# Inverses of the delta rule's triangular matrices: block levels on TensorE in place of a 16x16 substitution on VectorE through DRAM

## The chip, the cores and the metric

The kernel runs on one core of a Trainium2 chip. The metric is the device time of one execution in microseconds, the median of some runs. Profiles and traces show one execution. TensorE does the matrix products, VectorE (DVE), ScalarE (ACT) and GpSimd (POOL) the rest, and SyncE (SP) issues most transfers.

## The reference

One step of a backbone of two layers, for 512 latent tokens and 128 context tokens of width 1024. Each layer projects the normed tokens, runs four mixers side by side (grouped-query attention, neighbourhood attention, a gated delta rule in both directions, latent attention), projects their outputs and adds a gated feed-forward net of width 2816. The change is in the delta rule. It works on chunks of 64 tokens; for each chunk, head and direction a unit triangular system of 64x64 is solved:

```
def gated_delta_chunked(q, k, v, beta, logd, s0):
    c = DN_CHUNK                                   # 64
    ...
    gcum = jnp.cumsum(gc, axis=-1)
    dmask = jnp.where(tril, jnp.exp(jnp.where(tril, gcum[..., :, None] - gcum[..., None, :], 0.0)), 0.0)
    kb = kc * bc[..., None]
    a = jnp.where(strict, jnp.einsum('nbhid,nbhjd->nbhij', kb, kc) * dmask, 0.0)
    rhs = jnp.concatenate([vc * bc[..., None], kb * jnp.exp(gcum)[..., None]], axis=-1)
    sol = lax.linalg.triangular_solve(a + jnp.eye(c, dtype=jnp.float32), rhs,
                                      left_side=True, lower=True, unit_diagonal=True)
    u, w = sol[..., :dv], sol[..., dv:]
    ...
    def step(s, xs):
        u_i, w_i, qk_i, qd_i, kd_i, gl_i = xs
        v_new = u_i - jnp.einsum('bhcd,bhde->bhce', w_i, s)
        o_i = jnp.einsum('bhcd,bhde->bhce', qd_i, s) + jnp.einsum('bhij,bhje->bhie', qk_i, v_new)
        s = s * gl_i[..., None, None] + jnp.einsum('bhcd,bhce->bhde', kd_i, v_new)
        return s, o_i
    s_fin, o = lax.scan(step, s0.astype(jnp.float32), (u, w, qk, q_dec, k_dec, g_last))
```

There are 10 chunks, 4 heads and 2 directions, so 80 such matrices in each layer. The backward direction is the forward one on flipped tokens, so its matrices are upper triangular in the kernel's token order.

## The kernel before

All tokens stand side by side (640 columns) with features on 128 partitions. Large products take their operands in two parts of reduced precision, three products for one (L362, `mm3`; the loops at L624 to L711): these are the dense products, on full 128x128 blocks (tiles `acc` and `tacc` in the trace). Weights come in pieces through SP's queue and are split by ScalarE (`whi`) and VectorE (`wlo`).

TensorE's instructions are written out in an order that is fixed when the kernel is built. `_Order` (L190) keeps coroutines with ranks; each yields the time from which it can go on, an event, or buffers that it takes, and of those that can go on the first in rank does. `spend` keeps a measure of the dense columns issued of late (`heat`); while it is below a threshold, dense coroutines go first (L254 to L260). `via` estimates when a chain of steps on other engines ends. These are the planner's own estimates and serve the order alone. The other engines are ordered by the framework, each runs its instructions strictly one after another.

In a layer the mixer (L1850) spawns the delta rule's chain with rank 0 (`delta_chain`, L781), the other projections with rank 2 (`rest`, L1895), the modulation of layer 0 with rank 0.4 (`trickle`, L1924, transfers `wmd`, tiles `mpart`, `msb`), and the norms of the other mixers, which start at the event `inv` (L842). Attention (L1932) waits for the chain's end, since it takes over its room, and the half of the projections that is left runs beside it.

The chain: the keys' features and their short convolution (`conv_steps`, L735); the gates (L876); for 5 pairs of chunks the matrices `M` (tile `dM`) by L988 in `chunk_matrices` (L954), transposed, one head's parity on each half of the partitions; then the inverses; then the scan over the chunks (L1155) in both directions at once, and the output (`delta_out`, L1242). The values' and queries' features are projected meanwhile (L836, L837).

The inverses before: `inverse16` (L1014) writes the diagonal blocks of 16 of all matrices to DRAM (tile `dinv`, 8 transfers at L1025), reads them back with a whole matrix on each partition (L1034, L1035), turns the upper ones over (L1036), eliminates in 15 steps of two products and two subtractions on VectorE (L1043, L1047), and carries the inverses back through DRAM into the tile `rt` (L1049 to L1053). `inverse` (L1058) goes on with blocks in three groups of 8, 8 and 4 pairs of chunk and head: from 16 to 32 by two sets of 32x32 products (`first`, `second`: tiles `invp`, `ivr`, `ivy`), and from 32 to 64 by two sets (`third`, `fourth`) whose result replaces `M`. Before each first set VectorE turns `rt` over by 32x32 blocks (L1078). One coroutine runs the three groups one after another in each set.

Of the kernel before, what the change touches and what calls it, by code (L numbers as in the profile page):

```python
# [11 lines left out]
F32 = mybir.dt.float32  # L12
# [15 lines left out]
L = 2  # L28
# [24 lines left out]
def _constants():  # L53
# [6 lines left out]
    c["eye16"] = np.broadcast_to(np.eye(16, dtype=np.float32).reshape(1, 256), (128, 256))  # L60
# [3 lines left out]
    c["lev"] = np.stack([np.where((j < 16) & (i >= 16), -1.0, 0.0), np.where((j >= 16) & (i < 16), -1.0, 0.0)], 1)  # L64
# [23 lines left out]
_CBASE = ("ident", "ubig", "ident2", "eye16", "dmask", "lev", "sel2", "namask")  # L88
# [6 lines left out]
def _layout(inp):  # L95
# [25 lines left out]
    # gate columns ordered (parity, a|b, dir, pair)  # L121
# [47 lines left out]
    # state: (l, dir, parity, dk, pair, dv)  # L169
# [20 lines left out]
class _Order:  # L190
    """Order of the tensor engine's instructions among coroutines. A coroutine yields the time from which it can go on,
    an event, or (name, count) of the buffers that it takes; of those that can go on, the first in rank does.
    Times are estimates and only order instructions."""
# [82 lines left out]
class _Banks:  # L276
    """PSUM banks of some pools by turns: for every tag a list of (pool, tag)."""
# [10 lines left out]
class _Build:  # L288
# [13 lines left out]

    def split(self, hi, lo, src):
# [3 lines left out]
    def weights(self, src, shape, pool=None, bufs=2, parts=None):  # L307
        """A piece of a weight matrix, in its two parts."""
# [12 lines left out]
    def spare(e, l, pool, n):  # L321
        """Room for the two parts of a piece of the FFN's last weights, where its other buffers are free by then."""
# [13 lines left out]
    def put(self, oh, k, a, src, view=None):  # L336
        """Two parts of a piece of the mixers' outputs, from token a on."""
# [44 lines left out]
    def setup(self):  # L382
# [25 lines left out]
        for k, sh in _PAR.items():  # L408
# [21 lines left out]
            "inv": self.dp.tile([L, 2, 2, 2, 20, 4, 256], F32, name="dinv"),  # L430
        }

# [53 lines left out]
    def modulate(self, f, pool):  # L486
        """A part of the modulation numbers left, by the vector engine: layer 0's last gate, then layer 1's."""
# [26 lines left out]
    def scales(self, l, which, ks=slice(0, KD)):  # L514
        """norm gain * (1 + scale) of a sub-layer."""
# [8 lines left out]
    def sumsq(self, x, k, hf, pool, i=None, eng=None):  # L524
        """Squares of feature tile k of one half of the tokens, added up (by GpSimd: but for the last)."""
# [13 lines left out]
    def rstd(self, hf, pool):  # L539
        """1 / rms of the tokens of a half (None: of all), on partitions."""  # L540
# [12 lines left out]
    def bcast(self, hf, r, ps):  # L553
        """The same on all partitions in PSUM: (group, first and last token, numbers)."""
# [5 lines left out]
    def norm_k(self, l, which, hf, k, x, rb, h, pool):  # L560
        """Feature tile k of a half, normed and modulated, in two parts."""
# [20 lines left out]
    def out_k(self, k, x, rb):  # L582
        """Feature tile k of a half, normed, to the output."""
# [9 lines left out]
    def hooked(gen, hooks):  # L593
        """A coroutine run through, with calls after some of its steps."""
# [11 lines left out]
    def plain(gen):  # L606
        """A coroutine run through at once."""
# [16 lines left out]
    def fm_group(self, srcs, rhs, ks, acc, ws=None, tags=("w", "w")):  # L624
        """Some fm_tiles, side by side over the contraction."""
# [45 lines left out]
    def half_steps(self, w, rhs, ks, h, acc, tag="fd"):  # L671
        """A half of an fm_tile, in one PSUM bank."""
# [108 lines left out]
    def delta_chain(self, l, h, S, dn, dt, ps, pd, first):  # L781
# [57 lines left out]
        for e in evs:  # L839
            yield e  # L840
# [1357 lines left out]
```

## Time and profile before

| | |
|---|---|
| time, median of 3 runs | 1983.79 us (1981.31 to 1987.83) |
| span of the profiled execution | 1987.7 us |
| TensorE busy | 1861.4 us, 94% |
| VectorE, ScalarE, GpSimd busy | 55%, 37%, 14% |
| mean granted clock of TensorE | 0.968 of 2.4 GHz |
| delta rule's chain, from a layer's blocks going to DRAM (L1025) to the last product of the inverse | 114.2 to 244.2 us in layer 0, 1097.6 to 1210.0 us in layer 1 |

Busy time is the sum of an engine's instructions; the granted clock is the share of full speed that TensorE had, which is at one of two levels at a time (2.4 and 1.2 GHz), so that a mean between 0.5 and 1 is a mix. Idle time before an instruction is given with what ended it.

### The profile page before, as it was taken

The numbers are of one execution on the slowest core, as the hardware profiler recorded it, in microseconds if no ns is written. First come the engines' busy times: TensorE is split into PE (matmuls) and PEld (weight loads), VectorE is DVE, ScalarE is ACT, GpSimd is POOL, SyncE is SP. The second block draws the span as 40 slices with busy tenths as digits, with TensorE's granted clock in tenths as the row PEclk, the third lists the DMA queues.
The fourth block names the chain that finished last, engine by engine and source line by source line (L and its number), as shares of the span: only waits on it lengthen the run. The fifth ranks groups of instructions, "written<-read, shape, count | busy, mean of one in ns | idle before, by whom it ended". The sixth has DMA issues, their size and how long they took to land.

```text
span 1987.7 us, 40377 instructions
## 1 busy us (share of the span) xinstructions
PE 1861.4 (94%) x16620; PEld 1756.2 (88%) x16620; DVE 1098.9 (55%) x2372; ACT 734.1 (37%) x1505; POOL 287.1 (14%) x470
## 2 busy tenths in 40 slices
PE   5988998899999999999999879889999999999997
PEld 4977787778899999999998878777889999999997
DVE  6565556677667557657565664567766232323344
ACT  4622123766542112212345323267655221221231
POOL 1120321233310000000033031123322000000001
PEclk9988799999999999999999898989999999999999
DMA  7334333142535435435422222213352222222231
GB/s 295 128 97 126 114 99 109 30 109 78 168 140 173 141 111 183 145 125 182 132 93 90 63 68 68 77 52 75 94 167 83 76 76 78 78 69 83 74 96 54
DMA packets 116520, 213.51 MB, mean 107 GB/s; under 512 B 44400, under 2 KB 64368, under 8 KB 116208
## 3 DMA queue, kind: packets, MB, share of 16 engines
q1 hardware_dynamic: 113520, 206.22, 33.0%
q0 software_dynamic: 2816, 4.72, 1.2%
q8 instruction: 130, 2.13, 0.4%
q14 instruction: 54, 0.44, 0.1%
HBM read 186.29 MB, written 19.89 MB: 104 GB/s over the span
## 4 chain that ended last, share of the span: by engine, by line
PE 76%; DVE 9%; DMA 6%; ACT 4%; issue 2%; POOL 1%; SPq 1%; DVEq 0%; ACTq 0%; POOLq 0%
PE acc L347 54%; PE tacc L347 6%; PE ptp L359 2%; PE pvo L347 2%; PE sc L347 2%; DVE wlo L305 1%; PE mpart L347 1%; PE invp L347 1%; DMA wst<-wout 1%; DMA ivw<-dinv 1%; ACT whi L304 1%; DMA wmd<-wmod 1%; ACT p L1284 1%; DMA wmd<-wmodT 1%; POOL ar L1423 1%
## 5 line engine op out<-in xcount | busy, mean ns | idle before, releaser
L347 PE MATMUL acc<-h,whi 128*128 128x256 f32 (+1 forms) x3520 | 683.7, 313 | 2.3 <-ACT h L570 1.4
L347 PEld LDWEIGHTS acc<-h,whi 128*128 128x128 f32 x3520 | 583.4, 191 | 10.0 <-issue 3.4
L304 ACT CAST whi<-wst 128x1024 fp32r<-128x1024 f32 (+3 forms) x210 | 203.5, 970 | 698.2 <-PE acc L347 654.5
L347 PE MATMUL acc<-h,wlo 128*128 128x256 f32 (+1 forms) x1760 | 415.4, 313 | 7.5 <-DVE wlo L305 7.5
L305 DVE TENSOR_TENSOR wlo<-wst,whi 128x1024 fp32r<-128x1024 f32 (+3 forms) x210 | 238.0, 1134 | 200.4 <-ACT whi L304 199.3
L347 PEld LDWEIGHTS acc<-h,wlo 128*128 128x128 f32 x1760 | 322.6, 191 | 10.7 <-DVE wlo L305 8.6
L347 PE MATMUL acc<-g,whi 128*128 128x256 f32 (+1 forms) x1128 | 216.7, 309 | 0.2 <-DVE g L305 0.2
L347 PEld LDWEIGHTS acc<-g,whi 128*128 128x128 f32 x1128 | 185.9, 188 | 0.4 <-DVE g L305 0.4
L537 POOL TENSOR_TENSOR sq<-sq 128x256 f32<-128x256 f32 (+1 forms) x48 | 48.7, 1014 | 923.8 <-ACT sq L531 923.3
L1800 DVE SCALAR_TENSOR_TENSOR x<-acc,mods,x 128x256 f32<-128x256 f32 (+1 forms) x144 | 55.6, 434 | 186.6 <-PE acc L347 186.5
L503 DVE SCALAR_TENSOR_TENSOR wmj<-wmd,cb 128x1024 f32<-128x1024 f32 x112 | 136.8, 1221 | 37.9 <-DMA wmd<-wmodT 36.6
L347 PE MATMUL tacc<-whi,h 128*128 128x256 f32 (+1 forms) x640 | 154.2, 322 | 1.4 <-issue 1.0
L347 PE MATMUL acc<-g,wlo 128*128 128x384 f32 (+1 forms) x564 | 135.2, 309 | 0.0
L347 PEld LDWEIGHTS tacc<-whi,h 128*128 128x128 f32 x640 | 114.7, 200 | 10.6 <-issue 6.2
L347 PE MATMUL acc<-oh,whi 128*128 128x384 f32 (+1 forms) x512 | 114.2, 313 | 1.9 <-DVE xe L1800 1.9
L359 PE MATMUL ptp<-cbase,p 128*128 128x128 f32 x512 | 82.1, 287 | 24.9 <-ACT pt L1319 13.4
L347 PEld LDWEIGHTS acc<-g,wlo 128*128 128x128 f32 x564 | 103.3, 188 | 0.0
L347 PE MATMUL tacc<-wlo,h 128*128 128x256 f32 (+1 forms) x320 | 100.2, 313 | 1.8 <-DVE wlo L305 1.8
L2116 DVE TENSOR_TENSOR sg<-acc,sg 128x256 f32<-128x256 f32 x88 | 39.2, 485 | 102.2 <-PE acc L347 102.2
L359 PEld LDWEIGHTS ptp<-cbase,p 128*128 128x128 f32 x512 | 57.7, 143 | 41.4 <-ACT pt L1319 16.8
L1284 ACT ACTIVATE p<-sc,sm 128x768 f32<-128x768 f32 (+1 forms) x96 | 79.8, 832 | 31.2 <-DVE sm L1281 23.0
L1287 POOL TENSOR_SCALAR dg<-cbase,sd 128x128 f32<-128x128 f32 x96 | 60.1, 627 | 204.7 <-DVE sd L1285 143.7
(322 smaller groups left out, 2655.5 us busy)
## 6 DMA issues: line engine op xcount, KB each, us to landing
wmd<-wmodT SPq DMA_DIRECT2D x56, 512.0 KB, 4.4
wst<-wg SPq DMA_DIRECT2D x44, 512.0 KB, 3.6
wst<-wu SPq DMA_DIRECT2D x44, 512.0 KB, 3.6
wmd<-wmod SPq DMA_DIRECT2D x40, 512.0 KB, 4.6
wst<-wd SPq DMA_DIRECT2D x34, 448.0 KB, 3.3
wst<-wfm SPq DMA_DIRECT2D x24, 512.0 KB, 4.3
wst<-wd SPq DMA_DIRECT2D x16, 512.0 KB, 3.5
wst<-wout SPq DMA_DIRECT2D x28, 256.0 KB, 3.1
```

Of the source, the lines that this page charges most:

```text
L304: self.nc.scalar.copy(hi, src)
L305: self.nc.vector.tensor_tensor(out=lo, in0=src, in1=hi.bitcast(F32), op=ALU.subtract)
L347: self.nc.tensor.matmul(out, lhsT, rhs, start=start, stop=stop)
L359: self.nc.tensor.transpose(out, in_, self.ident)
L503: nc.vector.scalar_tensor_tensor(out=j, in0=st, scalar=1.0, in1=self.cb[:, g], op0=ALU.mult, op1=ALU.mult, accum_out=self.msum[:, e, g:g + 1])
L537: (eng or nc.gpsimd).tensor_tensor(out=self.sq[hf][0], in0=self.sq[hf][0], in1=sq, op=ALU.add)
L1284: nc.scalar.activation(p, s, AF.Exp, bias=m, accum_out=d)
L1287: nc.gpsimd.tensor_scalar(out=dg, in0=self.ident, scalar1=d, scalar2=None, op0=ALU.mult)
L1423: nc.gpsimd.tensor_tensor(out=x[:, a:b], in0=x[:, a:b], in1=g.unsqueeze(1).to_broadcast([128, b - a, 64]), op=ALU.mult)
L1800: self.nc.vector.scalar_tensor_tensor(out=x_out[:, a:b], in0=o[h][:, a - HB * h:b - HB * h], scalar=m[:, 8 * gate + e, grp:grp + 1], in1=x ...
L2116: nc.vector.tensor_tensor(out=sg[:, s], in0=ou[q], in1=sg[:, s], op=ALU.mult)
```

## The change

The substitution and its two trips through DRAM go, with the tile `dinv`. The inverses are built by doubling blocks: the inverse of a block of 2s follows from those of its two halves of s and the block between them. A first step brings the four diagonal blocks of 32 to the products' result with four wide products per group, masks the entries next to the diagonal and adds the identity: that is the inverse by blocks of 2. Four levels (s = 2, 4, 8, 16) follow, each with a transposition on VectorE, a set of 32x32 products with `M`, a masked product on VectorE, a second set of 32x32 products and an addition on VectorE. The last level, from 32 to 64, is as before, except that GpSimd copies the diagonal blocks. Each of the three groups is now a coroutine of its own with rank 0, which starts when the matrices of its chunks are there. The masks `lev` grow from one level to five. In `mla_norm` the planner's time of the wait is changed, and two scalings on VectorE are kept in program order.

The diff, without comments that it drops:

```
-    c["eye16"] = np.broadcast_to(np.eye(16, dtype=np.float32).reshape(1, 256), (128, 256))
+    c["eye32"] = np.tile(np.eye(32, dtype=np.float32), (4, 1))
...
+    def in_turn(self, ins):
+        return self.tc.keep_in_program_order(ins)
...
         ev_m = od.spawn(self.query_matrices(qk, evs + [ev_q], pd), 0.7)
+        groups = ((0, 8, evs[0:2]), (8, 16, evs[2:4]), (16, 20, evs[4:5]))
+        inv = [od.spawn(self.inverse(i, a, b, e, dt, pd), 0) for i, (a, b, e) in enumerate(groups)]
         for e in evs:
             yield e
-        rt = self.inverse16(l, dt)
         S["inv"].at = od.now
-        yield od.via(("DMA", 9.0), ("DVE", 12.0)) + 4.0
-        S["back"].at = od.now
-        yield od.via(("DMA", 9.0))
-        yield od.spawn(self.inverse(rt, dt, pd), 0)
-        S["whole"].at = od.now
+        for e in inv:
+            yield e
...
-    def inverse16(self, l, dt):
...
-    def inverse(self, rt, dt, ps):
...
+    def inverse(self, g, a, b, evs, dt, ps):
         nc, od = self.nc, self.od
+        for e in evs:
+            yield e
+        n = b - a
+        sh = [128, 2, n, 32]
+        M = self.M.rearrange("p d n q c -> p d (n q) c")[:, :, a:b]
         quads = [slice(32 * q, 32 * q + 32) for q in range(4)]
         cols = [slice(32 * (q % 2), 32 * (q % 2) + 32) for q in range(4)]
+        rt = dt.tile(sh, F32, name=f"rt{g}")
...
+        us = 0.14 + 64 * n / 960
+        yield "dn", 1
+        zp = bank()
+        for p, c in zip(quads, cols):
+            self.mm(zp[p], self.eye32[p], M[p, :, :, c])
+        nc.vector.tensor_tensor(out=rt, in0=zp, in1=level(0), op=ALU.mult)
+        t = od.via(("DVE", us))
+        od.give("dn", at=t)
+        nc.vector.tensor_tensor(out=rt, in0=rt, in1=self.eye32.unsqueeze(1).unsqueeze(1).to_broadcast(sh), op=ALU.add)
+        t = od.via(("DVE", us), at=t)
+        for s in range(1, 5):
+            yield t
+            yield "ta", 1
+            r, y = work()
+            nc.vector.transpose(out=flat(r), in_=flat(rt))
+            yield od.via(("DVE", us))
+            yield "dn", 1
+            yp = bank()
             for d in range(2):
+                for i in range(n):
+                    for p, c in zip(quads, cols):
+                        self.mm(yp[p, d, i], M[p, d, i, c], r[p, d, i])
+            nc.vector.tensor_tensor(out=y, in0=yp, in1=level(s), op=ALU.mult)
+            t = od.via(("DVE", us))
+            od.give("dn", at=t)
+            yield t
+            yield "dn", 1
+            zp = bank()
             for d in range(2):
+                for i in range(n):
                     for p in quads:
+                        self.mm(zp[p, d, i], y[p, d, i], rt[p, d, i])
+            nc.vector.tensor_tensor(out=rt, in0=rt, in1=zp, op=ALU.add)
+            t = od.via(("DVE", us))
+            od.give("dn", at=t)
+            od.give("ta", at=t)
+        yield t
...
+        for p, c in zip(quads, cols):
+            nc.gpsimd.tensor_copy(M[p, :, :, c], rt[p])
...
-            yield od.now + 8.0
+            yield od.now + 6.0
             for q, (a, b) in enumerate(((0, 256), (256, 384))):
-                nc.vector.tensor_scalar(out=cr[:, a:b], in0=cr[:, a:b], scalar1=r[:, t, q:q + 1], scalar2=None, op0=ALU.mult)
+                self.in_turn(nc.vector.tensor_scalar(out=cr[:, a:b], in0=cr[:, a:b], scalar1=r[:, t, q:q + 1], scalar2=None,
+                                                     op0=ALU.mult))
+            yield od.via(("DVE", 0.7)) + 2.0
```

## Rows read from the trace of the kernel before

**Rows 1.** The page's first part: busy us (share) and instructions.
```profile
PE 1861.4 (94%) x16620; PEld 1756.2 (88%) x16620; DVE 1098.9 (55%) x2372; ACT 734.1 (37%) x1505; POOL 287.1 (14%) x470
```

**Rows 2.** Windows of layer 0: busy time (count) by engine, granted clock, DMA, GB/s.
```profile
core 0: us, PE busy (x) PEld busy (x) DVE busy (x) ACT busy (x) POOL busy (x), PEclk, DMA share, GB/s
131.00:150.00 19.00, 14.01 (x79) 13.14 (x78) 18.34 (x58) 6.23 (x14) 0.34 (x6) 0.73 0.25 86
166.00:178.00 12.00, 8.29 (x101) 6.86 (x96) 0.86 (x3) 2.00 (x4) 0.00 (x0) 0.72 0.49 103
...
205.00:220.00 15.00, 11.27 (x137) 8.73 (x134) 12.93 (x26) 1.86 (x3) 10.52 (x18) 0.77 0.40 120
220.00:250.00 30.00, 30.00 (x424) 26.42 (x423) 10.63 (x28) 7.83 (x23) 2.71 (x8) 0.66 0.33 99
250.00:330.00 80.00, 79.41 (x1169) 68.89 (x1167) 44.03 (x144) 20.23 (x49) 15.34 (x38) 1.00 0.27 84
330.00:345.00 15.00, 8.41 (x50) 6.65 (x45) 9.54 (x17) 10.43 (x19) 2.44 (x4) 0.89 0.69 206
```

**Rows 3.** Windows of layer 1, the same columns.
```profile
1106.00:1125.00 19.00, 12.77 (x68) 12.51 (x67) 13.52 (x54) 2.39 (x7) 0.17 (x3) 0.73 0.10 36
1143.00:1158.00 15.00, 7.32 (x120) 6.68 (x117) 4.98 (x13) 2.55 (x6) 0.00 (x0) 0.77 0.35 61
1158.00:1187.00 29.00, 27.52 (x812) 25.44 (x812) 23.09 (x56) 8.21 (x21) 17.76 (x30) 1.00 0.28 78
1187.00:1215.00 28.00, 25.50 (x396) 24.27 (x394) 13.81 (x35) 6.59 (x19) 2.11 (x6) 0.70 0.21 67
...
1278.00:1315.00 37.00, 24.38 (x232) 20.13 (x227) 24.72 (x58) 19.58 (x37) 4.98 (x9) 0.72 0.30 89
```

**Rows 4.** Timeline: start, length, instruction, [idle before <- what ended it].
```profile
131.56 1.06 DVE L1036 COPY ivx<-ivw 40x1024 f32<-40x1024 f32 x1 [8.57 <-DMA ivw<-dinv]
138.73 2.29 PE L347 MATMUL ssp<-cbase,convy 128*128 128x2 f32 x10 [4.99 <-ACT convy L753]
171.69 1.08 PE L347 MATMUL mpart<-wmd,sc 128*32 128x256 f32 x8 [3.71 <-DMA wmd<-wmod]
1152.57 1.97 PE L347 MATMUL tokp<-cbase,convin 64*64 64x64 f32 x32 [7.68 <-DVE ss L761]
```

**Rows 5.** Instructions of a tile or line: count, shortest/median/longest ns, first and last start.
```profile
L1043 DVE TENSOR_TENSOR ivw<-ivv,ivx x60: 180/252/286, 133.5 to 1133.5; 104x30 f32<-104x30 f32 x8, 104x56 f32<-104x56 f32 x8, 104x78 f32<-104x78 f32 x8, 104x96 f32<-104x96 f32 x8
L1100 DVE TENSOR_TENSOR ivz<-invp,cbase x6: 411/678/684, 203.3 to 1189.3; 128x512 f32<-128x512 f32 x4, 128x256 f32<-128x256 f32 x2
```

**Rows 6.** Tile `invp`, then TensorE's timeline through the old level of layer 1.
```profile
L347 PE MATMUL invp<-ivr,dM x960: 184/191/258, 179.8 to 1201.3; 32*32 32x32 f32 x192
...
1159.12 1.29 PE L347 MATMUL invp<-ivr,dM 32*32 32x32 f32 x128
...
1171.10 0.74 PE L347 MATMUL invp<-ivr,dM 32*32 32x32 f32 x64 [1.39 <-DVE ivr L1078]
...
1181.12 0.46 PE L347 MATMUL acc<-h,whi 128*128 128x256 f32 x2
1181.50 0.75 PE L347 MATMUL invp<-rt,ivy 32*32 32x32 f32 x64
1182.18 0.56 PE L347 MATMUL acc<-h,whi 128*128 128x256 f32 x2
```

**Rows 7.** Timeline: a full product of 512 columns, and the last level's first piece.
```profile
109.82 1.02 PE L347 MATMUL decp<-decay,cbase 128*128 128x512 f32 x2
...
1190.23 2.98 PE L347 MATMUL invp<-ivr,dM 32*32 32x32 f32 x64 [2.50 <-DVE ivr L1078]
```

**Rows 8.** VectorE's timeline in layer 1: matrices of the first and the last group.
```profile
1085.26 0.69 DVE L988 TENSOR_TENSOR dM<-gram,dQ 128x512 f32<-128x512 f32 x1 [0.70 <-ACT dQ L977]
...
1093.18 0.69 DVE L988 TENSOR_TENSOR dM<-gram,dQ 128x512 f32<-128x512 f32 x1 [1.10 <-PE gram L347]
```

More of the change, by code (lines that the diff above doesn't have):

```diff
@@ L63, in _constants @@
     j, i = (p % 32)[:, None], np.arange(32)[None, :]
-    c["lev"] = np.stack([np.where((j < 16) & (i >= 16), -1.0, 0.0), np.where((j >= 16) & (i < 16), -1.0, 0.0)], 1)
+    lev = []
+    for s in (1, 2, 4, 8, 16):
+        pair = j // (2 * s) == i // (2 * s)
+        jl, il = j % (2 * s) < s, i % (2 * s) < s
+        low, high = (-1.0 * (pair & m) for m in (~jl & il, jl & ~il))
+        lev.append((high, low) if s == 1 else (low, high))
+    c["lev"] = np.array(lev).transpose(2, 0, 1, 3)
     c["sel2"] = np.stack([(p % 32 == 0), (p % 32 == 1)], 1).astype(np.float32)
@@ L85, in _constants @@
     return {k: np.ascontiguousarray(v, dtype=np.float32) for k, v in c.items()}
-_CBASE = ("ident", "ubig", "ident2", "eye16", "dmask", "lev", "sel2", "namask")
+_CBASE = ("ident", "ubig", "ident2", "eye32", "dmask", "lev", "sel2", "namask")
 _CROPE = ("cosA", "sinA", "cosK", "sinK", "cosM", "sinM")
@@ L429, in setup @@
             "lat": self.dp.tile([L, 4, 128, T], F32, name="dlat"),
-            "inv": self.dp.tile([L, 2, 2, 2, 20, 4, 256], F32, name="dinv"),
         }
@@ L1012, in query_matrices @@
         yield t
-    def inverse16(self, l, dt):
-        nc = self.nc
-        Z = self.dscr["inv"][l]
-        rt = dt.tile([128, 2, 20, 32], F32, name="rt")
-        nc.gpsimd.memset(rt.rearrange("p d b c -> p (d b c)"), 0.0)
-        M = self.M.rearrange("p d n q c -> p d (n q) c")
-        for r in range(2):
-            for q in range(4):
-                p = slice(64 * r + 16 * q, 64 * r + 16 * q + 16)
-                nc.sync.dma_start(out=Z[0, r, :, :, q].rearrange("d b (j i) -> j (d b) i", j=16),
-                                  in_=M[p, :, :, 16 * q:16 * q + 16].rearrange("p d b i -> p (d b) i"))
-        def t(name):
-            return self.ta(dt, name, 1024).rearrange("p (q j i) -> p q j i", q=4, j=16)
-        X, V, W = t("ivx"), t("ivv"), t("ivw")
-        S = W
-        nc.gpsimd.memset(X.rearrange("p q j i -> p (q j i)"), 0.0)
-        nc.sync.dma_start(out=X[0:40].rearrange("p q j i -> p (q j i)"), in_=Z[0, :, 0].rearrange("r b q e -> r b (q e)"))
-        nc.sync.dma_start(out=S[64:104].rearrange("p q j i -> p (q j i)"), in_=Z[0, :, 1].rearrange("r b q e -> r b (q e)"))
-        nc.vector.tensor_copy(X[64:104], S[64:104].rearrange("p q j i -> p q i j"))
-        nc.gpsimd.tensor_copy(V.rearrange("p q j i -> p q (j i)"), self.eye16.unsqueeze(1).to_broadcast([128, 4, 256]))
-        p = slice(0, 104)
-        for j in range(15):
-            sh = [104, 2, j + 1, 15 - j]
-            qs = (slice(0, 2), slice(2, 4))
-            for q in qs:
-                nc.vector.tensor_tensor(out=W[p, q, 0:j + 1, 0:15 - j], in0=V[p, q, 0:j + 1, j:j + 1].to_broadcast(sh),
-                                        in1=X[p, q, j:j + 1, j + 1:16].to_broadcast(sh), op=ALU.mult)
-            for q in qs:
-                v = V[p, q, 0:j + 1, j + 1:16]
-                nc.vector.tensor_tensor(out=v, in0=v, in1=W[p, q, 0:j + 1, 0:15 - j], op=ALU.subtract)
-        nc.vector.tensor_copy(S[64:104], V[64:104].rearrange("p q j i -> p q i j"))
-        nc.sync.dma_start(out=Z[1, :, 0].rearrange("r b q e -> r b (q e)"), in_=V[0:40].rearrange("p q j i -> p (q j i)"))
-        nc.sync.dma_start(out=Z[1, :, 1].rearrange("r b q e -> r b (q e)"), in_=S[64:104].rearrange("p q j i -> p (q j i)"))
-        for r in range(2):
-            for q in range(4):
-                nc.sync.dma_start(out=rt[64 * r + 16 * q:64 * r + 16 * q + 16, :, :, 16 * (q % 2):16 * (q % 2) + 16]
-                                  .rearrange("p d b i -> p (d b) i"),
-                                  in_=Z[1, r, :, :, q].rearrange("d b (j i) -> j (d b) i", j=16))
-        return rt
@@ new lines, in inverse, with flat, work, bank @@
+        rt = dt.tile(sh, F32, name=f"rt{g}")
+        def flat(t):
+            return t.rearrange("p d b c -> p (d b c)")
+        def work():
+            t = dt.tile([128, 1024], F32, tag="ta", name="ivw", bufs=3)
+            return [t[:, 64 * n * i:64 * n * i + 64 * n].rearrange("p (d b c) -> p d b c", d=2, c=32) for i in range(2)]
+        def bank():
+            return ps.tile(sh, F32, tag="dn", name="invp")
+        def level(s):
+            return self.lev[:, s].unsqueeze(2).to_broadcast(sh)
@@ new lines, in inverse @@
+        yield t
+        yield "ta", 1
+        r, y = work()
+        nc.vector.transpose(out=flat(r), in_=flat(rt))
+        yield od.via(("DVE", us))
+        yield "dn", 1
+        yp = bank()
+        pairs = [(d, q, quads[2 * q + d], quads[2 * q + 1 - d]) for d in range(2) for q in range(2)]
+        for d, _, e, o in pairs:
+            for i in range(n):
+                self.mm(yp[o, d, i], M[e, d, i, cols[1 - d]], r[e, d, i])
+        for d, q, _, o in pairs:
+            if q:
+                nc.vector.tensor_copy(y[o, d], yp[o, d])
+            else:
+                nc.scalar.copy(y[o, d], yp[o, d])
@@ new lines, in inverse @@
+        t = od.via(("ACT", 0.8))
+        od.give("dn", at=t)
+        for p, c in zip(quads, cols):
+            nc.gpsimd.tensor_copy(M[p, :, :, c], rt[p])
+        yield t
+        yield "dn", 1
+        zp = bank()
+        for d, _, e, o in pairs:
+            for i in range(n):
+                self.mm(zp[e, d, i], y[o, d, i], rt[o, d, i])
+        for d, q, e, _ in pairs:
+            out = M[e, d, :, cols[1 - d]]
+            if q:
+                nc.scalar.mul(out, zp[e, d], -1.0)
+            else:
+                nc.vector.tensor_scalar(out=out, in0=zp[e, d], scalar1=-1.0, scalar2=None, op0=ALU.mult)
@@ L1155, in scan @@
+        t = od.via(("ACT", 0.8))
+        od.give("dn", at=t)
+        od.give("ta", at=t)
+        yield t + 0.5
     def scan(self, steps, s, S, dn, ps, seen=()):
```

80 lines of the change are left out of this document (removed).

## The prediction

> **What bounds the kernel now.** I read the page's busy times first: TensorE works 94% of the span, no other engine over 55% [rows 1]. So a microsecond taken from VectorE or from a queue counts only where TensorE waits for it, and a microsecond put on TensorE counts in full wherever TensorE is not waiting anyway. The next view is the windows, stretch by stretch, with busy time and granted clock side by side. I use one measure: what a stretch loses is its length minus TensorE's busy time times the granted clock. In the scan of layer 0 that is 0.6 us of 80, so the planner can hide a long chain of small steps behind dense products almost perfectly [rows 2]. The losses of the delta rule's stage lie elsewhere:
>
> - around the DRAM trip: 131 to 150 loses 19 - 14.01 x 0.73 = 8.8 us and 166 to 178 loses 6.0; in layer 1, 1106 to 1125 loses 9.7 and 1143 to 1158 loses 9.4 [rows 2, 3]. Together 33.9 us;
> - 205 to 220, 6.3 us [rows 2];
> - the last level (blocks of 32 to the whole), 220 to 250 and 1187 to 1215, 10.2 us each, nearly all of it because the granted clock is 0.66 and 0.70 there, a mix of 2.4 and 1.2 GHz [rows 2, 3];
> - the end of the chain, where the dense products have run out: 330 to 345 loses 7.5 us and 1278 to 1315 loses 19.4 [rows 2, 3].
>
> The third view, the timeline, says why the first kind is there. VectorE takes its instructions in order. The copy of the blocks that come back from DRAM stands 8.57 us waiting for its transfer, the short convolution of the queries stands behind it, and TensorE's next product waits 4.99 us for that convolution; the transfer back blocks VectorE a second time in layer 1, and TensorE waits 7.68 us for a small copy queued behind it; in layer 0 a weight transfer of the modulation comes 3.71 us late while the blocks are carried [rows 4].
>
> **What goes.** Both DRAM trips of a layer, with 20 transfers on SP's queue, the 30 products (60 in both layers [rows 5]) and as many subtractions on VectorE at some 0.25 us, about 15 us of VectorE a layer, two copies and three fills. With the trip go the waits behind it. I take all four stretches: -33.9 us. The bounds are -23 (the idle time alone, length minus busy: 5.0 + 3.7 + 6.2 + 7.7, if the clock is low there for other reasons) and -34. Those 15 us of VectorE by themselves count nothing: VectorE is not the bound. What is late next is VectorE's own chain, below.
>
> **What comes on TensorE.** The old kernel has one level by blocks inside the 32 (16 to 32) and the last one; the new one has four of the first kind (2 to 32), the last one, and a first step of 4 wide products per group. A level is 2 x 160 products of 32x32, as 2 x 3 pieces of 64, 64 and 32. The trace has 960 records for 480 products, two for each, and 128 records, one piece of 64, take 1.29 us when the four quadrants take turns; a piece of 32 takes 0.74 to 0.75 [rows 6]. A level is then 4 x 1.29 + 2 x 0.74 = 6.6 us. A pair of dense products takes 0.46 us in a run and 0.56 behind a piece [rows 6], and about as much is lost ahead of it: 0.2 us for each of six pieces, 1.2 us. Three more levels: 23.5 us a layer. The first step does not occur in the trace. The nearest row is a full product of 512 columns, 1.02 us [rows 7]: if the four quadrants run beside one another, as they do in the pieces, three groups cost 1.0 + 1.0 + 0.5 = 2.6 us with 0.6 for the changes; one after another, 10. I take 3.2, by the pieces. Sum 26.7 a layer, **+53 us**; upper bound +67. All of it counts, since TensorE has other work throughout.
>
> **What comes on VectorE.** Per group and level a transposition, a masked product and an addition, each near the 0.68 us of the masked product of a group of 8 [rows 5]: three more levels, about 16 us a layer, as much as the substitution gives back. Off TensorE's path, if dense work lies between. The copies of the diagonal blocks go to GpSimd; the scan needs them only later, so nothing, as long as they are not queued behind the queries' norms there (10.5 us busy of 15 at 205 to 220 [rows 2]), which would hold the scan's first products by that much. The scalings of the latent attention are pinned to program order on VectorE; no row prices that, I take nothing, within one wait of 5 us as in [rows 4] either way. But each wait of TensorE in the chain is one more point at which its fixed order can stand still, with all dense products queued behind. In the old level of layer 1, 1158 to 1187 loses 1.5 us, of which 1.39 is one such wait [rows 3, 6]. Three more levels at that rate are 4.5 us a layer, +9; from below the scan's rate says 0 and from above the old inverse's two waits, 1.39 and 2.50 us for 12 points [rows 6, 7], 0.32 us each: the new chain has 11 points per group, 33 a layer, so 42 more in all, 13 us with the clock intact and about twice that if it falls after them. I take +6, between the level's rate and the scan's, because the planner puts dense work between the pieces there as here.
>
> **What moves.** The groups start when their own chunks are there. In layer 1 the matrices of the first group are written by 1085.9 and the last by 1093.9 [rows 8], so the chain begins 8 us sooner. The old level takes 23.1 us from 1159.1 to 1182.2, six pieces with dense products between [rows 6]; four of them are 92 us, with the first step about 95. They stand in place of the 65 us of trip (1093.9 to 1159.1) and the 23 us of one level: 7 us more, 8 us sooner begun. The inverse as a whole ends about when it did, but part of the dense work that filled the trip is left, since the waits behind it are gone. I take for the tail what the 8 us are worth: -6 of 7.5 in layer 0 and -12 of 19.4 in layer 1 (8 us and the low clock behind them), -18; bounds -27 and +10 (the dense products run out sooner than before). Of the 6.3 us at 205 to 220, where VectorE works off what the trip held up, -6; bounds 0 and -6. The last level keeps its order and its 20 us; bounds -10 and +10.
>
> **The sum.** +53 - 34 - 18 - 6 + 6 = +1. The profiled execution spans 1987.7 us, 3.9 over the median of the three runs and inside their range; the sum is one of differences, so it is put on the median: **1985 us**.
>
> **The Trainium skill against the trace.** A piece of 128 records in 1.29 us is a start every 10 ns [rows 6]. The Trainium skill, "TensorE: Matmul & The Clock Gate", section "Wait — 56ns, not 53.3ns?", says that matmuls never start closer than about 25 ns. By that floor the 1,920 added records of a layer would be 48 us and not 19, the sum +57 us; the trace does not bear it out for products that go round the quadrants.
>
> **The rivals.**
> - A clear gain. The waits at the new levels stay at nothing as in the scan, both tails go (-27), half of the last levels' loss goes because the three groups no longer reach them together (-10): 53 - 34 - 27 - 6 - 10 = -24, about 1960. For it: 0.6 us lost in 80 of scan [rows 2]. Against it: the old inverse did lose at its waits [rows 6, 7].
> - Slower: TensorE stands at the new VectorE steps. 42 more points where a late transposition or product holds up all that is queued. At 0.32 us each it is 13 us, with a fallen clock up to 26, I take 20; the chain is then late, so a third of the tail's gain at best (-6), and no gain at 205 to 220: 53 - 34 + 20 - 6 = +33, about 2017. It decides from 0.3 us a point on (12 us and not 6), where the forecast's +1 becomes more than 0.3% of the time. For it: VectorE is busy 12.9 of 15 us at 205 to 220 and 23.1 of 29 at 1158 to 1187 [rows 2, 3].
> - It does not do what it says: the levels take so many dense products that the chain is no earlier and the tails stay as they are: 53 - 34 - 6 + 6 = +19, about 2003.
> - The pieces run one after another, as in the last level, where 64 records take 2.98 us [rows 7]: 47 ns a record, 1,920 of them 89 us and not 19 a layer, +140, about 2124. Against it: the four quadrants are the innermost loop of the new levels, as in the fast pieces. (This is the way in which the page's floor would show; by it, 2041.)
>
> **Chances.** Forecast, 1970 to 1998: 0.41 (0.15 of it faster, 0.17 within, 0.09 slower). Clear gain 0.27. Waits at VectorE 0.19. Chain no earlier 0.11 (0.02 of it within, 0.09 slower). Slow pieces 0.02. So faster by over 0.3% (6 us, about what a measurement of this kernel can tell) 0.42, within 0.19, slower 0.39. The range runs from 1950, a little past the clear gain, to 2020, past the waits. Cases of both signs hold most of the chance; the forecast's own range is 1970 to 1998.
>
> **What would show it.** The DRAM waits of [rows 4] gone and nothing in their place; some 960 x 2 more records a layer, 128 of them in 1.3 us, and TensorE busy about 50 us longer less what it now spends at the lower clock; no wait over 0.5 us at the inverse's products; the inverse's end within 10 us of 1210 in layer 1; less than 10 us lost in the tail of layer 1. Wrong if TensorE waits for VectorE at many of the new points, if the granted clock falls through the levels, or if the dense products are gone before the scan ends.

## The result and the profile after

The changed kernel takes 2045.1 us (median of four runs, 2041.1 to 2050.1), the kernel before beside it 1985.8: a ratio of 1.030, 95% interval 1.026 to 1.034. The forecast was 1985 with a range to 2020; it was wrong, and by more than any rival but the one at 0.02 allowed (2017 at most).

The page of the changed kernel: span, busy times with their instruction counts, the granted clock in 40 slices, and the queue that carries TensorE's instructions (transfers, MB, share).

```profile
span 2042.0 us, 47980 instructions
PE 1920.0 (94%) x20508; PEld 1802.4 (88%) x20508; DVE 1107.6 (54%) x2278; ACT 731.8 (36%) x1499; POOL 292.3 (14%) x488
...
PEclk8997799999999999999999979989999999999999
...
q8 instruction: 161, 2.64, 0.5%
```

Against [rows 1] TensorE is busy 58.6 us longer, in 3,888 more records: 960 x 2 a layer and 48 of the first step, as forecast. I split every span in windows of 1 us and add up three things: *work* (busy time x granted clock), *idle* (length minus busy time), and *clock* (busy time x what the clock lacks). Lost is idle plus clock, the forecast's measure. Before: work 1811, idle 126, clock 50, lost 177. After: work 1864, idle 122, clock 56, lost 178. So the work came as forecast in sum (+53), and the losses, which were to shrink by 52, did not shrink at all.

Where they lie now: windows of the changed kernel (length, busy time of PE, PEld, DVE, ACT, POOL with records, granted clock, DMA share, GB/s). The first three answer to [rows 2], the last two to [rows 3].

```profile
143.00:171.00 28.00, 20.68 (x1025) 15.73 (x1028) 12.32 (x21) 3.10 (x7) 0.00 (x0) 0.59 0.31 98
...
206.00:240.00 34.00, 29.56 (x767) 24.32 (x760) 16.27 (x48) 2.86 (x8) 2.42 (x4) 0.60 0.25 80
...
260.00:345.00 85.00, 82.63 (x1184) 73.86 (x1179) 56.52 (x169) 25.57 (x63) 33.33 (x68) 1.00 0.26 78
...
1190.00:1222.00 32.00, 28.24 (x847) 26.85 (x848) 18.06 (x34) 3.81 (x9) 7.76 (x16) 0.70 0.05 15
...
1340.00:1380.00 40.00, 30.11 (x257) 25.42 (x254) 26.56 (x51) 28.01 (x61) 7.53 (x12) 0.87 0.27 85
```

143 to 171 alone loses 28 - 20.68 x 0.59 = 15.8 us, 206 to 240 loses 16.3, 1190 to 1222 loses 12.2. These are stretches of the new levels. 260 to 345 holds layer 0's tail and loses 2.4. The last line is layer 1's tail, still there: 40 - 30.11 x 0.87 = 13.8 us, where the forecast left 7.4. What TensorE waits for in the whole kernel (in all, times, longest):

```profile
PE invp L358 <- issue: 18.4, 15, 2.7
...
PE invp L358 <- DVE ivw L1099: 2.9, 4, 1.1
...
PE invp L358 <- DVE ivw L1071: 1.8, 3, 0.7
```

Of the waits of [rows 4], those for the blocks, for the convolution and for the copy behind them are gone. Those of the modulation for its weights are not: without the first one of the kernel they were 6.0 us in three and are 6.7 us in five, none over 1.9. The rival's waits for VectorE are some 5 us. The large entry is one that neither the forecast nor a rival had: the products of the inverse wait for "issue", 18.4 us. The timeline shows where (start, us, operation, records, and in brackets the idle time ahead):

```profile
134.74 1.20 PE L358 MATMUL invp<-rt,ivw 32*32 32x32 f32 x119
137.80 0.34 PE L358 MATMUL invp<-rt,ivw 32*32 32x32 f32 x9 [1.86 <-issue]
138.07 1.08 PE L358 MATMUL mpart<-wmd,sc 128*32 128x256 f32 x8
...
142.96 1.29 PE L358 MATMUL invp<-ivw,dM 32*32 32x32 f32 x128
...
147.44 1.47 PE L358 MATMUL invp<-rt,ivw 32*32 32x32 f32 x109 [0.87 <-issue]
150.67 1.08 PE L358 MATMUL mpart<-wmd,sc 128*32 128x256 f32 x8 [1.76 <-DMA wmd<-wmod]
151.68 1.93 PE L358 MATMUL invp<-ivw,dM 32*32 32x32 f32 x128
...
159.78 1.05 PE L358 MATMUL invp<-rt,ivw 32*32 32x32 f32 x63
163.18 1.11 PE L358 MATMUL invp<-rt,ivw 32*32 32x32 f32 x65 [2.35 <-issue]
```

A piece stops in its middle, where nothing has to come but its own instructions. After the stop at 137.8 the same eight products of the modulation take 1.08 us where they took 0.64 at 131.6: the clock has gone to the lower of its two levels (1.2 and 2.4 GHz), and from 147 on a piece of 64 takes 1.93 us and not 1.29. The transfers on the instruction queue, each of 16,384 bytes, fit the stops one by one; seven of them, in us from the span's start:

```
block landed     136.59  146.01  154.05  157.59  161.74  165.24   1137.05
piece goes on    137.80  147.44  155.45  158.90  163.18  166.63   1138.41
stop (us)          1.86    0.87    0.64    0.44    2.35    0.44      2.72
```

There are 16 such stops of over 0.4 us in the stretches of the two inverses, 18.9 us together, and every one ends 1.2 to 1.5 us after a block has landed. The trace has 41,232 instructions of TensorE, its waits for semaphores included, to 161 transfers: 256 each. Counted through from the start, the number of instructions started before a stop leaves 193 on division by 256, at all 16 stops, and at all 40 stops of over 0.4 us in the traces of the other kernels. So TensorE stops at one place only, where a block of 256 ends. The shortest distance between two such transfers in the whole trace is 3.30 us. A product of 32x32 is two MATMUL and two LDWEIGHTS records, so a piece of 64 is 256 instructions, as many as one block. A piece takes 1.29 us of the array and at least 3.3 us of supply.

### The profile page after: what moved, and what is told of

The parts are those of the page before. It is cut to its first block, busy times and chain, and to the rows that moved or that the text cites. A ratio compares the mean times of both kernels' runs of the same rounds, so it can differ in the third digit from the quotient of the medians.

```text
span 2042.0 us, 47980 instructions
## 1 busy us (share of the span) xinstructions
PE 1920.0 (94%) x20508; PEld 1802.4 (88%) x20508; DVE 1107.6 (54%) x2278; ACT 731.8 (36%) x1499; POOL 292.3 (14%) x488
## 4 chain that ended last, share of the span: by engine, by line
PE 81%; DVE 8%; DMA 4%; ACT 4%; issue 3%; POOL 0%; SPq 0%; DVEq 0%; ACTq 0%; POOLq 0%
PE acc L358 56%; PE tacc L358 7%; PE invp L358 3%; PE sc L358 2%; PE pvo L358 2%; PE ptp L370 2%; PE mpart L358 1%; DMA wmd<-wmod 1%; DVE wlo L316 1%; ACT p L1252 1%; ACT whi L315 1%; DVE sm L1249 1%; PE ysp L358 1%; DVE nq L1730 1%; PE tokp L358 1%
## 5 line engine op out<-in xcount | busy, mean ns | idle before, releaser
L358 PE MATMUL tacc<-whi,h 128*128 128x256 f32 (+1 forms) x640 | 147.1, 311 | 0.5 <-ACT whi L315 0.5
L358 PEld LDWEIGHTS tacc<-whi,h 128*128 128x128 f32 x640 | 107.9, 188 | 6.9 <-issue 1.2
L1252 ACT ACTIVATE p<-sc,sm 128x768 f32<-128x768 f32 (+1 forms) x96 | 79.8, 831 | 35.0 <-DVE sm L1249 27.7
```

What stands on the lines that cost most here:

```text
L358: self.nc.tensor.matmul(out, lhsT, rhs, start=start, stop=stop)
L1252: nc.scalar.activation(p, s, AF.Exp, bias=m, accum_out=d)
```

## Experiments

Three theories stood after the two traces: A, the supply of instructions; B, the products cost their array time and the trip was worth little; C, the order: the inverses share three PSUM banks with the short convolutions, and the dense products come too late. The kernel before took 1984.1, 1989.8, 1991.0 and 1985.9 us beside the four groups of experiments, so ratios are to the kernel before beside each run. *Idle*, *clock*, *work* and *lost* are of the profiled execution.

**One level only.**

```
-        for s in range(1, 5):
+        for s in range(4, 5):
```

> The changed kernel with only the level 16 to 32, the last level and the first step left; the levels 2, 4 and 8 are left out. Against the kernel before it has the same levels on TensorE and no DRAM trip, so it tells what the trip's going away is worth. The forecast's own terms (-34 for the trip's waits, -18 for the tails, -6 for 205 to 220, +6 for the first step) say 1985 - 52 = 1934 us. Theory A (instruction supply: TensorE's small products come at most some 75 instructions a us, so a piece of 64 needs 3.5 us, not 1.29): the 24 pieces of 64 and 12 of 32 that are left out cost up to 3.5 and 1.75 us each, 105 us, so 1940. Theory B (the added products cost their array time only, 40 us for these levels, and the trip was worth nearly nothing): 2005. Theory C (the three inverses take the PSUM banks from the short convolutions, so dense products come late): the three levels left out take their share of the hold with them, 1965 to 1985.

1954.7 us, ratio 0.985 (0.979 to 0.990). Work 1823, idle 101, clock 33, lost 134. So without the trip and without the added levels 43 us of losses are gone, where the forecast's terms say 58 (34 + 18 + 6) and 1934 us. The stages with the trip (100 to 260, 1060 to 1220) lose 39 us less, against 34 + 6; the stretches behind them (260 to 450, 1220 to 1420) lose 3 us less, against 18. The three levels back in (the changed kernel) are 41 us of work and **44 us of losses** beside it: 21 idle and 23 clock. B (2005) falls; A had said 1940 and C 1965 to 1985.

**No transfers in the kernel before.**

The 20 `dma_start` of `inverse16` are left out, X and S are filled with zeros after the last `dM`, and `rt` is filled from V.

> The kernel before, with the 20 transfers a layer of the blocks of 16 left out (the substitution runs on zeros); its order of work, its levels and its VectorE work stay. It measures the waits for the transfers by themselves. The forecast says -34 us (bounds -23 and -34): 1952. Theory B says within 10 us of the kernel before, 1975 to 1985, because the dense products held back fill later holes. Theories A and C say nothing here but the forecast's -23 to -34.

1946.6 us, 0.981 (0.976 to 0.985): -37 us, lost 132. Work is the same as before (1812).

```profile
span 1944.3 us, 40340 instructions
PE 1845.5 (95%) x16620; PEld 1742.0 (90%) x16620; DVE 1099.9 (57%) x2372; ACT 735.1 (38%) x1505; POOL 296.6 (15%) x500
```

The same 16,620 records as in [rows 1], and 16 us less busy time: that is the time they took at the lower clock. The stages with the trip lose 44 us less, the stretches behind them 3 more. So the forecast's -34 for the trip and -6 at 205 to 220 were right in sum, and nothing of its -18 for the tails shows here.

**The inverses behind the convolutions.**

```
-        inv = [od.spawn(self.inverse(i, a, b, e, dt, pd), 0) for i, ...
+        inv = [od.spawn(self.inverse(i, a, b, e, dt, pd), 0.1) for i, ...
```

> The changed kernel with the three inverses at rank 0.1, not 0, so that the short convolutions of the queries and values get the three PSUM banks first. Theory C: the dense products come back into 143 to 171 of layer 0, the granted clock with them, and 15 to 40 us are saved: 2005 to 2030. Theory A: the pieces still come at the supply's pace, 0 to 10 us saved: 2035 to 2045. Theory B: 2045.

2033.2 us, 1.024 (1.020 to 1.029). The dense products of `acc` in 143 to 171, first in the changed kernel, then with the rank (columns: length, busy PE, PEld, DVE, ACT, clock, DMA):

```profile
143.00:171.00 28.00, 0.03 (x1) 0.00 (x0) 0.00 (x0) 0.81 (x3) 0.59 0.31 98
```

```profile
143.00:171.00 28.00, 17.25 (x92) 14.97 (x92) 0.00 (x0) 1.61 (x6) 0.94 0.40 133
```

So C is right for the place of the dense products in this stretch: the changed kernel has no dense product there, with the rank there are 17 us of them, and the clock is 0.94 and not 0.59. The stages of the inverses (100 to 260, 1060 to 1300) lose 35 us instead of 71. But the stretches behind them (260 to 600, 1300 to 1600) lose 89 instead of 65: the dense products that fill the inverse are missing in the scan's tail. 12 us are left of 36 (by the medians; the two intervals overlap, the single runs do not).

**Few wide products in the same order.**

```
-            for d in range(2):
-                for i in range(n):
-                    for p, c in zip(quads, cols):
-                        self.mm(yp[p, d, i], M[p, d, i, c], r[p, d, i])
+            for p, c in zip(quads, cols):
+                nc.tensor.matmul(yp[p], M[p, 0, 0, c], r[p], start=True, stop=True)
+            for i in range(8 * n):
+                od.spend(0.035, 4)
```

> The changed kernel with every piece of 32x32 products of the levels 2 to 32 put in one wide product per quadrant (512 or 256 columns; 16 instructions and not 256), the planner being told the old durations so that the order of all instructions stays nearly the same. The inverse is then not computed. A wide piece takes 1.06 us by the first step's row and a small one 1.29, so array time alone gives (1.29 - 1.06) x 64 pieces of 64 and half of that x 32 of 32, some 18 us less: theory B 2027. Theory A: with 96 pieces of 256 and 128 instructions fewer the instruction stalls go too, 20 to 50 us more: 1975 to 2007. Theory C: as B, 2020 to 2027, since banks and order are the same.

2001.0 us, 1.008 (1.006 to 1.011): 44 us less than the changed kernel. Only 6 of them are work, where I had expected 18; lost is 144 and not 178 (idle 112, clock 32). The order of TensorE's instructions is the same but for the pieces. No stop for instructions is left. The stretch that answers to 143 to 171, up to the same dense product:

```profile
138.00:159.00 21.00, 13.60 (x124) 3.62 (x122) 11.89 (x21) 3.33 (x7) 0.00 (x0) 0.93 0.41 135
```

The pieces have no dense products between them here either, and TensorE even waits more for weights; the stretch is over in 21 us at a clock of 0.93. The clock stays at its upper level for most of it, first line; in the changed kernel it is at the lower one from 148 to 171, second line:

```profile
138.00:156.00 18.00, 11.05 (x108) 3.23 (x106) 11.89 (x21) 3.33 (x7) 0.00 (x0) 1.00 0.47 154
```

```profile
148.00:171.00 23.00, 17.25 (x762) 12.98 (x756) 8.18 (x16) 1.57 (x3) 0.00 (x0) 0.50 0.31 94
```

So the want of dense products does not bring the clock down by itself: without them TensorE is busy 11 of 18 us with e4_wide at the full clock, and 17 of 23 in the changed kernel at half of it.

**Two blocks a product: 128 instructions a piece.**

```
+                for i in range(0, n, 2):
+                    for p, c in zip(quads, cols):
+                        nc.tensor.matmul(yp[p, d, i:i + 2], M[p, d, i, c], r[p, d, i:i + 2], start=True, stop=True)
```

> The changed kernel with each two neighbouring 32x32 products of the levels 2 to 32 put in one product of 64 columns (the first one's weights for both): 128 instructions a piece of 64 and not 256, the same columns, the planner told the same durations. The inverse is then not computed. With the measured fetches of 256 instructions at best every 3.3 us, a piece then needs 1.7 us of supply and its array time is some 1.1 to 1.2. Theory A (supply): most of what e4_wide gained comes here too, 2003 to 2018, and the stops for instructions (19 us in the changed kernel, none in e4_wide) fall under 5 us. A theory that every instruction costs the same small time gives half of the 44 us: 2023. Theory C (banks and order): 2040, as order and banks are the same.

2014.2 us, 1.014 (1.010 to 1.018); lost 149 (idle 108, clock 40), no stop for instructions. Half the instructions give 29 of the 34 us of losses back, and 31 of 44 us by the medians; a fixed price for each instruction would give a little over half (128 of 240).

**Both.** e4_wide with the rank 0.1 of e3_rank.

> e4_wide (16 instructions a piece) with the inverses at rank 0.1 as in e3_rank. If order and banks are a cause of their own (theory C), the 12 us of e3_rank come on top of the 44: 1989. If e3_rank gained only because its pieces came less densely and so ran short of instructions less (its stops for instructions are 11 us and not 19), nothing is left to gain: 1998 to 2003.

2004.5 us, 1.008 (1.005 to 1.012), lost 143 against 144. Clock falls from 32 to 22, idle rises from 112 to 120. Once the instructions are few, this change of the order gives nothing.

**The number of instructions put back with the wide shape.**

```
+            for i in range(2 * n - 1):
+                for p, c in zip(quads, cols):
+                    nc.tensor.matmul(yp[p, 0, 0, 0:2], M[p, 0, 0, c], r[p, 0, 0, 0:2], start=True, stop=True)
```

and, for 128 instructions, `range(n - 1)`.

> e4_wide (2001, same order as the changed kernel, wide products) with 60 tiny products of 2 columns ahead of each wide one, written over by it: 256 instructions a piece again, as in the changed kernel, but other products. Their array time has no row; 120 more records at no more than 10 ns each are up to 1.2 us a piece, 0 to 90 us for all, and it is read from TensorE's work at full clock. What counts is the time lost beside that work. Theory A (supply): it goes from e4_wide's 144 back to 165 to 180 (178 in the changed kernel), and the stops for instructions come back, each ending 1.2 to 1.5 us after a block of instructions has landed, 15 to 40 us in all. If it was the shape of the products and not their number that cost the 34 us, lost time stays at 140 to 150 and there are no stops.

> The same with 28 tiny products, 128 instructions a piece, as in e4b_two. Theory A: lost time 144 to 155, stops under 5 us, as there. If every instruction costs the same, half of what e13_pad256 loses.

256 instructions: 2066.2 us, 1.039 (1.035 to 1.044), lost 174 (idle 108, clock 65). 128: 2027.8 us, 1.0215 (1.018 to 1.025), lost 148 (idle 107, clock 41). So the loss rises with the number: 144, 148, 174 for 16, 128 and 256 with wide products, 149 and 178 for 128 and 256 with narrower ones. With the wide products the array time of a piece rises too, from 1.06 to 2.1 us, and work from 1858 to 1892, so these two runs alone do not part the number from the length. And I expected 15 to 40 us of stops, and there are 4.8 us in seven: a padded piece asks for instructions less densely. What grew is the clock's part, 32, 41, 65. The stretch with no dense product between the pieces:

```profile
146.00:177.00 31.00, 27.73 (x945) 13.89 (x937) 10.93 (x20) 1.57 (x3) 0.00 (x0) 0.63 0.33 105
```

It lasts 31 us at 0.63, busy 27.7 us of them. So theory A in its narrow form, the time of the stops alone, does not carry the loss: what costs most is that such a stretch becomes longer and runs at the lower clock. The stops still stand where it falls. In the stages of the inverses the granted clock falls seven times in this kernel, five of them during a stop or within 2 us of its end (each 0.3 to 0.9 us), two behind waits of 2.4 and 3.7 us for VectorE. In the changed kernel it falls seven times, six of them so, one behind a wait of 1.9 us for weights; in e4_wide four times, behind waits for weights and VectorE.

**Hiding the trip in the kernel before.** The substitution planned 15 us after its transfers, the inverse 16 us after the transfers back, with and without pins on VectorE.

```
+        yield self.od.via(("DMA", 15.0))
+        self.tc.keep_in_program_order(nc.vector.tensor_copy(X[64:104], ...
...
-        yield od.via(("DMA", 9.0), ("DVE", 12.0)) + 4.0
-        yield od.via(("DMA", 9.0))
+        yield od.via(("DVE", 15.0), ("DMA", 16.0))
```

> The kernel before, its inverse through DRAM kept and complete, but the planner is told 15 and 16 us for the two transfers (9 each before; the trace shows 15.6 and 15.9 from the last write to the first read), the substitution is planned after the first transfer and not at its issue, and the copy and the transpositions that read what comes back are pinned on VectorE behind all that was planned before them. e2_no_transfers says that the waits are worth 37 us. If they come from VectorE's order (what stands behind the waiting copy), most of it is had without removing the trip: 1950 to 1965. If they come from the chain being later for want of other work, nothing is gained: 1980 to 1995.

> e8_later without the pins: only the planner's times. If the place of the copy on VectorE is what matters and the times alone set it, as e8_later: 1950 to 1965. If the scheduler of VectorE still puts the copy ahead of the convolutions, the waits stay: 1975 to 1990.

1.002 (0.9995 to 1.004) and 1.002 (1.000 to 1.004): nothing. Waits of VectorE with the pins:

```profile
DVE mcr L1547 <- DMA mcr<-dcraw: 22.4, 6, 9.6
...
DVE ivx L1036 <- DMA ivw<-dinv: 8.4, 1, 8.4
```

Much of them moved from the blocks to the loads of the latent attention (in the kernel before 16.7 us for the copy L1036 and 6.0 for `mcr<-dcraw`).

> e8_later with the times that its trace shows (21 us from the last write to the copy, 20 back; 22 and 20 told), and with the changed kernel's part of the latent attention's norm: its scalings pinned on VectorE and 6 us after their loads. In e8_later the waits had moved to the copy (8.4 us), to the transpositions (5.5 and 6.2) and to these scalings (18 us of VectorE). If the waits can be hidden with the trip kept, 1950 to 1970. If the chain, now some 15 us later, loses in the tail what it gains, 1975 to 1990.

1.001 (0.9985 to 1.003). Layer 1's stretch with the trip (1060 to 1220) now loses 12 us and not 33, but layer 0's stretch from 250 to 360 28 and not 12, and layer 1's from 1220 to 1400 33 and not 27. From the last write of `dM` to the scan's last `otp` the two layers take 217 and 200 us before, 219 and 198 with e8_later, 231 and 185 with e9_later2: the sums are equal, and so are the times. With no transfers they are 194 and 181, 43 us less, beside the 44 us less lost. So in these kernels time goes with the length of the chain, and hiding the trip's waits behind dense products takes these away from the tail. That the chain's length is the cause is not shown: with e3_rank it is 457 us in both layers and 448 in the changed kernel, and e3_rank is the faster one.

**The norm's part alone, and undone.** The change also pins the scalings of the latent attention and puts them 6 us after their loads.

> The kernel before with one part of the change alone: the scalings of the latent attention's norm pinned and 6 us after their loads. The forecast took nothing for it, within one wait of 5 us. A part of the trip's waits may hang on these scalings (VectorE stands up to 10 us for their loads): then 1970 to 1980.

> The changed kernel with this part undone: the scalings right behind their loads, not pinned. Forecast: 2045, within 5 us. If the pinning is what keeps VectorE free in the changed kernel, 2050 to 2065.

In the kernel before: 0.9953 (0.9936 to 0.9970), some 9 us **faster than both kernels**; from the last `dM` to the last `otp` the layers take 210 and 195 us, 13 less together. VectorE's waits for these loads, before and with this part:

```profile
DVE mcr L1547 <- DMA mcr<-dcraw: 6.0, 4, 3.4
...
DVE mcr L1547 <- DMA mcr<-crope: 4.9, 1, 4.9
```

```profile
DVE mcr L1548 <- DMA mcr<-crope: 2.7, 1, 2.7
```

Undone in the changed kernel: 1.025 (1.021 to 1.029) against 1.030 (1.026 to 1.034), not slower, rather 10 us faster in the profile (2032.2). There the pinning does not help; the intervals overlap.

**The planner told 55 ns a small product,** in e3_rank.

```
-            ... else (0.035, 0.47e-3)
+            ... else (0.055, 0.47e-3)
```

> e3_rank (2033) with the planner told 55 ns a small product and not 35: 64 of them 3.5 us, which is what a block of 256 instructions takes to arrive, so that it counts on the supply's pace. Theory A: the planner no longer takes operands to be late or early by the difference, 2015 to 2033. If order has no part in it (e34_wide_rank says so), 2028 to 2040.

2041.1 us, 1.026 (1.022 to 1.029), the same as e3_rank's 1.024. The stops for instructions fall from 11 us to 5, but lost rises from 166 to 182, 8 of these 16 us in longer waits of the scan's outputs and the modulation for VectorE. Fewer stops by another order are paid for elsewhere.

## Why the prediction was wrong, point by point

The losses were to fall by 52 us and rose by 1. Of these 53 us, 38 are missing in the step on the waits at the new points and 15 in the step on what moves.

- *What comes on TensorE, +53.* Right in sum, perhaps in part by luck: work +53. The forecast's three levels were 47 with their changes and the first step 6; measured are 41 for the levels and 12 for the rest (kernels with the same records as the changed one differ from it by up to 4 in work). A piece takes 1.29 us at the full clock. The first step's quadrants run beside one another as assumed; its row is 1.06 us for 512 columns on four quadrants.
- *What goes, -34, and the -6 at 205 to 220.* Right: 40 forecast, 39 in e1_one_level, 44 in e2_no_transfers.
- *The waits at new points, +6.* **This step failed.** I priced the added levels beside their work by VectorE's lateness alone, with the scan's and the old level's loss as ends. VectorE's part was near that (5 us of waits). The losses beside the work are 44 us, over seven times the step. 34 of them go when pieces of the same columns, in the same order, have 16 instructions and not 256: 24 of the lower clock and 10 idle; 29 go with 128. I had read the pieces' 1.29 us from an inverse that had six in 23 us, with dense products between [rows 6]; I did not ask what feeds them when there are four times as many, nor whether enough dense products are left to stand between them. The rows of before had small products at a low clock: the last level ran at 0.66 and 0.70 [rows 2, 3], and I carried those 20 us along as a thing of that level. It is no plain sign of this loss, though, since it has dense products between its pieces (13.8 of 28 us in layer 1) and no stop for instructions.
- *What moves, -18.* **This step failed too.** The chain was to begin 8 us sooner and its levels to take 95 us. In layer 1 the first group's matrices are written by 1118.7 and the last by 1127.0, and the first step starts at 1125.8: 1 us sooner and not 8, in layer 0 as well (why, no run here shows). From there to the end of the fourth level it takes 130 us in layer 0 and 121 in layer 1, and still 110 and 102 with e4_wide. From the last `dM` to the last product of the inverse it takes 138 and 128 us and not 130 and 116. Layer 0's stretch from 260 to 345 did gain (2.4 us lost), but 360 to 400 behind it loses 12 and not 3; layer 1's tail gave 6 of its 12. Even without the added levels (e1_one_level) the tails gave 3 of the 18.
- *The latent attention's pins, nothing within 5 us.* Alone they are worth 9 us, in the changed kernel nothing or a loss.
- *The rivals.* Waits for VectorE at the new points (0.19) named the right step with the wrong cause. A chain that is no earlier (0.11) did happen, and accounts for the 15 us of the tails. "Slow pieces" (0.02) came out as wrong in its mechanism: 64 products take 1.29 us at the full clock, 10 ns a record. So the trace still does not bear out the 25 ns of the Trainium skill ("TensorE: Matmul & The Clock Gate", section "Wait — 56ns, not 53.3ns?"). The sum by that floor, 2041, is near the 2045 measured, but by another mechanism: luck.

The sum that was missing, an estimate from the rows of after: the 960 added products a layer are 3,840 instructions, 15 blocks of at least 3.3 us, 50 us of supply where I counted 20 of the array. The page has the 31 blocks (161 against 130 for both layers). Where dense products stand between the pieces the supply can run ahead under them (the stop at 137.8 comes in spite of them); where none are left, up to 30 us a layer come on top.

The Trainium skill, "Runtime: NRT & Kernel Launch", section "Instruction fetch mechanics", says that instructions come in blocks of 256, the next while the current ones run, and that the cost of crossing a block is mostly hidden. The blocks agree with the trace. Hidden the crossings were in the kernel before (1.0 us of stops), and not here (18.9 us).

**What stays open.** How the 24 us of clock divide between the stops and the want of dense products was not separated. e3_rank brings the clock back with dense products, e4_wide without them. Six of the changed kernel's seven falls come with a stop, but why the clock then stays low from 148 to 171, no run here shows. Why a piece goes on only 1.2 to 1.5 us after its block has landed, none shows either.

## What to carry to other kernels

Price small products on TensorE by two terms, array time and instructions: here four for each fp32 product of 32x32, 256 in at least 3.3 us, and add up the whole chain, not one piece. Dense products that hide a chain can be spent once; hiding the trip's waits without shortening the chain gave them back in the tail here. When a change has a small second part, time it alone: here that part, without the rest, was the faster kernel.

## What was not expected of the hardware

- TensorE's instructions came in transfers of 16,384 bytes, 256 instructions each, at best 3.30 us apart (five in a row in 17.8 us). Every stop for them stood at the same place of a block of 256, and a stopped piece went on 1.2 to 1.5 us after a transfer had landed.
- With no dense product the clock stayed at its upper level through 17 us of wide products and waits (e4_wide); among small ones it fell to the lower level right behind a stop of 0.87 us.
- 59 products of 32x32 with 2 columns (118 records, e13_pad256) took 1.14 us at the full clock, nearly as much as 64 with 32 columns (1.29): at that clock products of this size cost by their number.
